# Weight tiles and split buffers of a two-layer decoder: eleven raw tiles and four pairs for the experts, six pairs in the mixers and the dense stage

## The chip, the cores and the metric

The kernel runs on one core of a Trainium2 chip. A core has five engines with queues of their own: TensorE (PE in the profile; PEld are its weight loads, which overlap the matmuls), VectorE (DVE), ScalarE (ACT), GpSimd (POOL) and SyncE (SP), which here issues nearly all DMAs. Each queue runs in order: an instruction that waits holds up everything behind it on its engine. The metric is the time of one execution on the device, in microseconds (us); lower is better.

## The reference

Two layers of a decoder for 256 tokens with 1024 channels, all in float32. Each layer is a mixer stage and a feed-forward stage, each with a residual. What is computed, shortened:

```python
for l in range(2):
    h = rmsnorm(x, norm_mix[l])
    z = h @ w_in[l]                                   # 2816 columns, shared out among four mixers
    y_a, y_b, y_c, y_d = gmlp(z_a), pool(z_b), attention(z_q, z_k, z_v), conv(z_d)
    gates = sigmoid(h @ w_gate[l] + b_gate[l])        # 4 x 1024 columns
    merged = sum(gates[:, b] * (y_b @ w_br[b][l]) for b in "abcd")
    x = x + merged @ w_out[l]
    h = rmsnorm(x, norm_ffn[l])
    if l == 0: f = (silu(h @ w1) * (h @ w3)) @ w2     # dense, 2816 hidden
    else:      f = sum over 8 experts of combine[:, e] * ((silu(h @ w1[e]) * (h @ w3[e])) @ w2[e])
    x = x + f                                         # experts: 3584 hidden, the top 2 of 8 per token
out = rmsnorm(x, norm_final)
```

## The kernel before

**Weights.** All large weights come from HBM in tiles of 1024 KB (128 partitions x 2048 float32, 8 KB per partition), called raw. `load_raw` takes the next tile of a ring and has SP load it. `load_w` does the same and then splits each half of the tile into two parts, whi and wlo (128 x 1024 each): ScalarE copies the half into the reduced float format (`split`, L164), VectorE subtracts the copy from the original (L165). A whi and its wlo make a pair of buffers, also 8 KB per partition. A large product is then three matmuls in the reduced format: hi x whi, hi x wlo and lo x whi (`mm3`, L156 to L158), or two where both parts of the activations stand side by side (`both_parts`, L240 and L242). A raw tile is free again when its two halves are split, a pair when its last matmul is done.

**Rings.** `rawp` has 4 raw tiles (NRAW). The expert stage adds a pool `rawm` of NRAW_MOE = 5, so there its ring has 9. The pool `wp` has 6 pairs, which all stages share; every allocation takes the next of them.

**Stages.** `norm_T` normalises x, two tiles of 128 tokens one after the other (`norm_rows`: squares on ScalarE L200, their sum L201, root L202, reciprocal L204, scaling L207; with the residual's addition L199 ahead of them), and turns the result for TensorE (L217). `mixer_layer` works through 32 tiles of weights: the input projection, 16 gate units (psw), the branches a, b, d and c (psb). Branch c comes last: its two tiles, four pairs, are used for every block of output columns, so all four are held until its end; branch d, just before it, uses two pairs. While it runs, VectorE and ScalarE merge the branch into `merged` and split the result into mp (L564 to L569). `out_proj` follows with four tiles (pso, `rows_by_token_tile`): the first two are used up for both token tiles before the next; the last two are held until the first token tile is finished with both, so that its norm can begin early. `dense_ffn` has 33 tiles (psw for the up products, psf for the down product).

**Experts.** `moe` counts the tokens of each expert and sorts the experts by size. The four larger ones have room for 128 tokens and use split weights; the four smaller ones have room for 64 and multiply in plain float32 straight from the raw tiles, which are held until those matmuls are done. `paired` runs 28 steps, seven for each pair of a larger and a smaller expert. A step takes 12 raw tiles, in this order: two for the first up product of the large expert (psu, L866), two for the down product of the small one two steps back (psds, L944), two for the second up product, four for the small expert's up products (psq, L923; 32 matmuls), two for the large one's down product (psd). Between them stand gfm (L872, L873) and gfs (L925, L926), which apply the activation to psu and psq, and the transposes with their evacuations gTr, gTl and gTs. At each change of pair the inputs of the next two experts are gathered by matmuls (psg, L835), and the results are scattered back (L902). Which expert a tile belongs to is known in advance for the first one alone; for the others SP reads the number from SBUF (L1014) before it can issue the load.

**Order.** The program is traced in the order of the source; then a planner, which simulates the engines and the DMA with costs of its own, puts the instructions of each engine into the order in which they run in this simulation. A split can so run ahead of its place in the source, as soon as the planner believes its tile landed and its pair free. The order is fixed at build time. `hold_splits` (L110) keeps some splits after each norm behind the norm's last instructions; the first two halves are exempt (skip = 2).

**Memory.** Pools are stacked: a pool opened in a stage lies where the pools of the stage before it lay, and with reuse_waits="tile" each tile waits only for the tiles that lay in its place. A stage's pools are closed at its end.

The ring, and the two lines that choose a pair:

```python
ring = {"pools": [rawp] * NRAW, "i": 0, "skip": 0, "after": []}
    hi = wp.tile([P, a // 2, n], F32R, name="whi", tag="whi")
    lo = wp.tile([P, a // 2, n], F32R, name="wlo", tag="wlo")
ring.update(pools=[rawm] * NRAW_MOE + [rawp] * NRAW, i=0)      # in moe, L675
```

Of the kernel before, what the change touches and what calls it, by code (L numbers as in the profile page):

```python
# [11 lines left out]
F32R = mybir.dt.float32r  # L12
# [5 lines left out]
P = 128  # L18
# [11 lines left out]
WINDOWS = (2, 4, 8, 16)  # L30
NSLOT = 128
NRAW = 4
NRAW_MOE = 5
NSMALL = 64
RMS_EPS = 1e-6
LN_EPS = 1e-5
# [59 lines left out]
def decoder_kernel(ctx, tc, x_in, consts_in, mconsts_in, bias_in, small_in, gln_in, gbs_in, norms_in, w_in,  # L96
# [3 lines left out]
    cp = ctx.enter_context(tc.tile_pool(name="cp", bufs=1))  # L100
    actp = ctx.enter_context(tc.tile_pool(name="actp", bufs=1))
    rawp = ctx.enter_context(tc.tile_pool(name="rawp", bufs=NRAW))
    wp = ctx.enter_context(tc.tile_pool(name="wp", bufs=6))
    psA = ctx.enter_context(tc.tile_pool(name="psA", bufs=4, space=bass.MemoryType.PSUM))
    psB = ctx.enter_context(tc.tile_pool(name="psB", bufs=4, space=bass.MemoryType.PSUM))


    ring = {"pools": [rawp] * NRAW, "i": 0, "skip": 0, "after": []}

    def hold_splits(ins, skip):  # L110

# [2 lines left out]
    @contextmanager  # L114
    def behind(ins):
        with ExitStack() as st:
            for i in ins:
                st.enter_context(tc.issue_after(i.ins))
            yield

    def load_raw(src, a, n):
        pool = ring["pools"][ring["i"] % len(ring["pools"])]
        ring["i"] += 1
        raw = pool.tile([P, a, n], F32, name="raw", tag="raw")
        nc.sync.dma_start(raw, src)
        return raw

    def load_w(src, a, n):

        raw = load_raw(src, a, n)
        halves = []
        for i in range(2):
            r = raw[:, i * (a // 2):(i + 1) * (a // 2)]
            hi = wp.tile([P, a // 2, n], F32R, name="whi", tag="whi")
            lo = wp.tile([P, a // 2, n], F32R, name="wlo", tag="wlo")
            with behind(ring["after"] if -6 < ring["skip"] <= 0 else []):
                split(hi, lo, r)
            ring["skip"] -= 1  # L140
            halves.append((hi, lo))
        return halves, a // 2

    def wsl(wt, k, c0, n):
        halves, ah = wt
        return tuple(p[:, k % ah, c0:c0 + n] for p in halves[k // ah])

    def w_cols(w, c0, n):
        return load_w(w[:, c0:c0 + n].rearrange("(k p) n -> p k n", p=P), KD, n)

    def w_rows(w, k0, nk, c0=0, n=D):
        return load_w(w[k0 * P:(k0 + nk) * P, c0:c0 + n].rearrange("(k p) n -> p k n", p=P), nk, n)

    def mm3(ps, lhs, rhs, start, stop):

        nc.tensor.matmul(ps, lhsT=lhs[0], rhs=rhs[0], start=start, stop=False)  # L156
        nc.tensor.matmul(ps, lhsT=lhs[0], rhs=rhs[1], start=False, stop=False)  # L157
        nc.tensor.matmul(ps, lhsT=lhs[1], rhs=rhs[0], start=False, stop=stop)  # L158

    def sl(pair, *idx):  # L160
        return (pair[0][idx], pair[1][idx])

    def split(hi, lo, src):
        return (nc.scalar.activation(hi, src, AF.Copy),  # L164
                nc.vector.tensor_tensor(out=lo, in0=src, in1=hi.bitcast(F32), op=ALU.subtract))  # L165
# [21 lines left out]
    def sqrt_table(after, rows=slice(None)):  # L187

        junk = cp.tile([P, 1], F32, name="junk", tag="junk", bufs=2)
        nc.scalar.activation(junk[rows], after, AF.Sqrt, scale=0.0, bias=eps_l[rows])  # L190
# [53 lines left out]
    def w_pair(h, wt, c=0):  # L244

        out = []
        for b in range(2):
            ps = psA.tile([P, 2, T], F32, name="psw", tag="mm")
            for k in range(KD):
                both_parts(ps, wsl(wt, k, c + b * P, P), h[2], k, k == 0, k == KD - 1)  # L250
            out.append(ps)
        return out

    def addends(pool, ps, out=None):

        if out is None:
            out = pool.tile([P, 2, T], F32, name="sum", tag="sum", bufs=2)
        for b in range(2):
            nc.scalar.activation(out[:, b], ps[b][:, 1], AF.Copy)  # L259
            nc.vector.tensor_tensor(out=out[:, b], in0=out[:, b], in1=ps[b][:, 0], op=ALU.add)  # L260
        return out


    def mixer_layer(l, h):
        with ExitStack() as lctx:
            lp = lctx.enter_context(tc.tile_pool(name=f"lp{l}", bufs=1, reuse_waits="tile"))
            wk = lctx.enter_context(tc.tile_pool(name=f"wk{l}", bufs=2, reuse_waits="tile"))
            sm = lp.tile([P, S_END], F32, name="sm")
# [345 lines left out]
    def out_proj(l, mT):  # L614

        ps = [[psB.tile([P, 512], F32, name=f"pso{t}{n}", tag="ax") for n in range(2)] for t in range(TT)]
        sqrt_table(mT[1].bitcast(F32)[:, KD - 1, 0:1])
        def part(i, wt, t):
            for k in range(2):
                for n in range(2):  # L620
                    mm3(ps[t][n], sl(mT, slice(None), 2 * i + k, slice(t * P, (t + 1) * P)),
                        wsl(wt, k, n * 512, 512), i == 0 and k == 0, i == 3 and k == 1)

        rows_by_token_tile(part, lambda i: w_rows(w_out[l], 2 * i, 2), 4)
        return ps


    def dense_ffn(i, h):
        with ExitStack() as lctx:
            wk = lctx.enter_context(tc.tile_pool(name="wkf", bufs=2, reuse_waits="tile"))  # L630
            ps2 = [[psB.tile([P, 512], F32, name=f"psf{t}{n}", tag="ax") for n in range(2)] for t in range(TT)]
            nch = DFF // 256

            def part(c, wt, g, t):
                for k in range(2):
                    for n in range(2):
                        mm3(ps2[t][n], sl(g, slice(None), k, slice(t * P, (t + 1) * P)),
                            wsl(wt, k, n * 512, 512), c == 0 and k == 0, c == nch - 1 and k == 1)

            def up(c):  # L640
                p1 = addends(wk, w_pair(h, w_cols(dense_w1[i], c * 256, 256)))
                p3 = addends(wk, w_pair(h, w_cols(dense_w3[i], c * 256, 256)))
                sil = wk.tile([P, 2, T], F32, name="sil", tag="sil")
                nc.scalar.activation(sil, p1, AF.Silu)
                if c == nch - 1:
                    sqrt_table(sil[:, 0, 0:1])
                gf = wk.tile([P, 2, T], F32, name="gf", tag="gf")
                nc.vector.tensor_tensor(out=gf, in0=sil, in1=p3, op=ALU.mult)
                g = (wk.tile([P, 2, T], F32R, name="gr", tag="gr"), wk.tile([P, 2, T], F32R, name="gl", tag="gl"))
                split(g[0], g[1], gf)  # L650
                return g

            g = {0: up(0)}
            for c in range(1, nch):
                g[c] = up(c)
                if c < nch - 1:
                    wt = w_rows(dense_w2[i], 2 * (c - 1), 2)
                    for t in range(TT):
                        part(c - 1, wt, g[c - 1], t)
            last = [(c, w_rows(dense_w2[i], 2 * c, 2)) for c in (nch - 2, nch - 1)]  # L660
            for t in range(TT):
                for c, wt in last:
                    part(c, wt, g[c], t)
        return ps2


    def moe(i, norm_i, l, mT):
        with ExitStack() as lctx:
            rawm = lctx.enter_context(tc.tile_pool(name="rawm", bufs=NRAW_MOE, reuse_waits="tile"))
            st = lctx.enter_context(tc.tile_pool(name="stm", bufs=2, reuse_waits="tile"))  # L670
# [3 lines left out]
            ps = out_proj(l, mT)  # L674
            ring.update(pools=[rawm] * NRAW_MOE + [rawp] * NRAW, i=0)  # L675

# [186 lines left out]
            def up_large(e, c, j0, xl):  # L863
                ps = psA.tile([P, 512], F32, name="psu", tag="mm")
                wt = [load_w(tile_of(e, c, j0 + j, 4), 4, 512) for j in range(2)]
                for k in range(KD):  # L866
                    mm3(ps, sl(xl, slice(None), k), wsl(wt[k // 4], k % 4, 0, 512), k == 0, k == KD - 1)
                return ps
# [173 lines left out]
    for l in range(DEPTH):  # L1042
        mT = mixer_layer(l, norm_T(ps, 2 * l))
        if l % 2 == 0:
            ps = dense_ffn(l // 2, norm_T(out_proj(l, mT), 2 * l + 1))
        else:
            moe(l // 2, 2 * l + 1, l, mT)
# [36 lines left out]
def build(tc, ins, outs):  # L1084
    decoder_kernel(tc, *ins.values(), outs["0"])
# [16 lines left out]
```

## Time and profile before

| | |
|---|---|
| median of 3 runs | 1591.19 us (1590.26 to 1591.65) |
| the profiled execution, its own time | 1589.84 us |
| its span, first to last instruction | 1588.1 us |
| granted TensorE clock, mean | 0.988 |
| TensorE busy | 1531.3 us, 96% |
| VectorE, ScalarE busy | 977.8 us, 808.1 us |
| read from HBM | 472.17 MB |

One execution was recorded. A line such as "L165 DVE TENSOR_TENSOR wlo<-raw,whi" names the source line, the engine, the operation, and what it writes and reads; the time in brackets at the end of a timeline row is how long the engine sat idle before it, and what ended this. Matmuls overlap in the array, so their start times, not their durations, tell the pace.

### The profile page before, as it was taken

Reading aid. Unit: us, or ns where it says so; the run is one execution under the profiler, and the core shown is the slowest. Engines: PE = TensorE matmul, PEld = TensorE weight load, DVE = VectorE, ACT = ScalarE, POOL = GpSimd, SP = SyncE. Lnnn points to the kernel's source line nnn. Section 1 sums busy time; section 2 is a strip of 40 time slices with the busy share of each in tenths; the row PEclk is TensorE's granted clock in tenths of the full one; section 3 lists DMA queues with packets and bytes.
Section 4 is the critical chain, followed back from the end, with each engine's and each line's share of the span. In section 5 each row is a group of like instructions: output and inputs, shape, how many; then the busy total and the mean of one; then the engine's idle time right before and its main releaser. Section 6 shows DMA issues by size and latency. Waiting matters only on the chain.

```text
span 1588.1 us, 20024 instructions
## 1 busy us (share of the span) xinstructions
PE 1531.3 (96%) x7508; PEld 1065.8 (67%) x7508; DVE 977.8 (62%) x1291; ACT 808.1 (51%) x1184; POOL 20.8 (1%) x47
## 2 busy tenths in 40 slices
PE   6999999999899999899999999999999999999997
PEld 5888897888788889776555555555555555555553
DVE  5896776665679777765445655454645554654444
ACT  5577746555464865554434534344434453444342
POOL 2000000000100000000000000000000000000000
PEclk9999999999999999989999999999999999999998
DMA  9565555555565645479998989999999999899993
GB/s 324 189 192 181 173 181 173 187 188 190 186 199 167 198 160 196 163 307 376 421 407 371 413 343 421 400 413 374 385 372 403 404 408 373 365 417 405 398 390 141
DMA packets 134890, 474.61 MB, mean 299 GB/s; under 512 B 7744, under 2 KB 77376, under 8 KB 91776
## 3 DMA queue, kind: packets, MB, share of 16 engines
q1 hardware_dynamic: 132512, 466.65, 76.2%
q0 software_dynamic: 1984, 6.08, 1.2%
q8 instruction: 61, 1.00, 0.3%
q10 hardware_dynamic: 288, 0.52, 0.1%
q14 instruction: 45, 0.37, 0.1%
HBM read 472.17 MB, written 1.05 MB: 298 GB/s over the span
## 4 chain that ended last, share of the span: by engine, by line
PE 89%; DVE 4%; ACT 4%; issue 2%; DMA 1%; SPq 0%; DVEq 0%; ACTq 0%
PE psw L240 16%; PE psq L923 14%; PE psw L242 8%; PE psu L157 7%; PE psu L158 7%; PE psu L156 6%; PE psds L944 5%; PE psd L157 3%; ACT whi L164 3%; PE psd L158 3%; DVE wlo L165 3%; PE psd L156 2%; PE psg L835 2%; PE psf L156 1%; PE psf L158 1%
## 5 line engine op out<-in xcount | busy, mean ns | idle before, releaser
L165 DVE TENSOR_TENSOR wlo<-raw,whi 128x1024 fp32r<-128x1024 f32 x546 | 647.7, 1221 | 252.8 <-ACT whi L164 249.6
L164 ACT ACTIVATE whi<-raw 128x1024 fp32r<-128x1024 f32 x546 | 554.0, 1053 | 130.4 <-PE psw L240 40.1
L240 PE MATMUL psw<-hp,whi 128*128 128x512 f32 x1088 | 388.6, 400 | 0.6 <-DVE hp L165 0.6
L242 PE MATMUL psw<-hp,wlo 128*128 128x256 f32 x1088 | 307.0, 282 | 0.0
L240 PEld LDWEIGHTS psw<-hp,whi 128*128 128x128 f32 x1088 | 205.1, 188 | 52.8 <-issue 3.3
L923 PE MATMUL psq<-raw,xs 128*64 128x512 f32 x896 | 218.6, 596 | 0.0
L242 PEld LDWEIGHTS psw<-hp,wlo 128*128 128x128 f32 x1088 | 206.3, 190 | 2.1 <-issue 1.1
L157 PE MATMUL psu<-wlo,xer 128*128 128x512 f32 x448 | 183.4, 409 | 9.5 <-DVE wlo L165 9.5
L156 PE MATMUL psu<-whi,xer 128*128 128x512 f32 x448 | 179.6, 401 | 1.3 <-DVE x L902 1.2
L158 PE MATMUL psu<-whi,xel 128*128 128x512 f32 x448 | 176.1, 393 | 0.0
L923 PEld LDWEIGHTS psq<-raw,xs 128*64 128x64 f32 x896 | 65.3, 137 | 129.0 <-issue 128.7
L925 ACT ACTIVATE gfs<-psq 64x512 f32<-64x512 f32 x28 | 16.5, 591 | 251.7 <-PE psq L923 251.7
L157 PEld LDWEIGHTS psu<-wlo,xer 128*128 128x128 f32 x448 | 84.6, 189 | 64.0 <-issue 30.0
L156 PEld LDWEIGHTS psu<-whi,xer 128*128 128x128 f32 x448 | 84.8, 189 | 41.9 <-ACT whi L164 17.0
L944 PE MATMUL psds<-raw,gTs 128*64 128x512 f32 x448 | 110.8, 604 | 0.0
L926 DVE TENSOR_TENSOR gfs<-gfs,psq 64x512 f32<-64x512 f32 x28 | 19.4, 692 | 137.7 <-ACT gfs L925 137.7
L158 PEld LDWEIGHTS psu<-whi,xel 128*128 128x128 f32 x448 | 84.8, 189 | 15.3
L157 PE MATMUL psd<-wlo,gTr 128*128 128x512 f32 x224 | 92.3, 412 | 2.1
L158 PE MATMUL psd<-whi,gTl 128*128 128x512 f32 x224 | 88.1, 393 | 0.0
L259 ACT ACTIVATE sum<-psw 128x256 f32<-128x256 f32 x120 | 44.8, 374 | 67.0 <-PE psw L242 67.0
L156 PE MATMUL psd<-whi,gTr 128*128 128x512 f32 x224 | 75.4, 413 | 2.7 <-ACT whi L164 2.7
L872 ACT ACTIVATE gfm<-psu 128x512 f32<-128x512 f32 x28 | 16.7, 597 | 119.9 <-PE psu L158 119.9
(260 smaller groups left out, 1570.4 us busy)
## 6 DMA issues: line engine op xcount, KB each, us to landing
raw<-in_moe_w_dram SPq DMA_DIRECT2D x336, 1024.0 KB, 8.2
raw<-in_dense_w_dram SPq DMA_DIRECT2D x33, 1024.0 KB, 5.3
raw<-in_w_gate_dram SPq DMA_DIRECT2D x32, 1024.0 KB, 5.4
raw<-in_w_in_dram SPq DMA_DIRECT2D x22, 1024.0 KB, 5.6
raw<-in_w_out_dram SPq DMA_DIRECT2D x8, 1024.0 KB, 5.0
raw<-in_w_br_c_dram SPq DMA_DIRECT2D x4, 1024.0 KB, 5.5
s<-in_bias_dram POOLq DMA_DIRECT2D x16, 192.0 KB, 4.2
gain<-in_norms_dram SPq DMA_DIRECT2D x5, 512.0 KB, 4.9
```

The costliest lines, as they stand in the source:

```text
L156: nc.tensor.matmul(ps, lhsT=lhs[0], rhs=rhs[0], start=start, stop=False)
L157: nc.tensor.matmul(ps, lhsT=lhs[0], rhs=rhs[1], start=False, stop=False)
L158: nc.tensor.matmul(ps, lhsT=lhs[1], rhs=rhs[0], start=False, stop=stop)
L164: return (nc.scalar.activation(hi, src, AF.Copy), nc.vector.tensor_tensor(out=lo, in0=src, in1=hi.bitcast(F32), op=ALU.subtract))
L165: nc.vector.tensor_tensor(out=lo, in0=src, in1=hi.bitcast(F32), op=ALU.subtract))
L240: nc.tensor.matmul(ps.rearrange("p a t -> p (a t)"), lhsT=w[0], rhs=act[:, k].rearrange("p a t -> p (a t)"), start=start, stop=False)
L242: nc.tensor.matmul(ps[:, 1], lhsT=w[1], rhs=act[:, k, 0], start=False, stop=stop)
L259: nc.scalar.activation(out[:, b], ps[b][:, 1], AF.Copy)
L835: nc.tensor.matmul(ps[:, b, cs], lhsT=ht[part][:, t, k * P:(k + 1) * P], rhs=self.G[:, t].rearrange("p s n -> p (s n)")[:, cs], start=n == ...
L923: nc.tensor.matmul(ps[rows], lhsT=xs[:, kk], rhs=w[:, k], start=kk == 0, stop=kk == KD - 1)
L926: nc.vector.tensor_tensor(out=gf[HI], in0=gf[HI], in1=ps[HI], op=ALU.mult)
L944: nc.tensor.matmul(acc["s"][rows], lhsT=gT[:, 2 * j + k], rhs=w[:, k, n * 512:(n + 1) * 512], start=c == 0 and j == 0 and k == 0, stop=c = ...
```

## The change

The experts' pool of raw tiles grows from 5 to 7, so the ring there has 11 tiles instead of 9. The pool `wp` shrinks from 6 pairs to NW = 4. `mixer_layer` and `dense_ffn` each open a pool of two further pairs for as long as they run (`more_parts`), so the ring of pairs has 6 there and 4 elsewhere: in the experts and in both output projections. The position in the ring of pairs is now counted by `ring["n"]`, which starts at 0 when such a pool opens and when it closes. The memory is the same: two raw tiles take as much as two pairs.

```diff
-NRAW_MOE = 5
+NRAW_MOE = 7
+NW = 4
...
-    wp = ctx.enter_context(tc.tile_pool(name="wp", bufs=6))
+    wp = ctx.enter_context(tc.tile_pool(name="wp", bufs=NW))
...
-    ring = {"pools": [rawp] * NRAW, "i": 0, "skip": 0, "after": []}
+    ring = {"pools": [rawp] * NRAW, "i": 0, "skip": 0, "after": [], "parts": [wp] * NW, "n": 0}
+
+    def more_parts(lctx, name):
+
+        pool = lctx.enter_context(tc.tile_pool(name=name, bufs=2, reuse_waits="tile"))
+        ring.update(parts=[wp] * NW + [pool] * 2, n=0)
+        lctx.callback(lambda: ring.update(parts=[wp] * NW, n=0))
...
-            hi = wp.tile([P, a // 2, n], F32R, name="whi", tag="whi")
-            lo = wp.tile([P, a // 2, n], F32R, name="wlo", tag="wlo")
+            pool = ring["parts"][ring["n"] % len(ring["parts"])]
+            ring["n"] += 1
+            hi = pool.tile([P, a // 2, n], F32R, name="whi", tag="whi")
+            lo = pool.tile([P, a // 2, n], F32R, name="wlo", tag="wlo")
...
     def mixer_layer(l, h):
         with ExitStack() as lctx:
+            more_parts(lctx, f"wp{l}")
...
     def dense_ffn(i, h):
         with ExitStack() as lctx:
+            more_parts(lctx, "wpf")
```

## The prediction

> **What bounds the kernel now.** The page comes first: the span, the engines' busy time, and the slices.
>
> ```profile
> span 1588.1 us, 20024 instructions
> PE 1531.3 (96%) x7508; PEld 1065.8 (67%) x7508; DVE 977.8 (62%) x1291; ACT 808.1 (51%) x1184; POOL 20.8 (1%) x47
> PE   6999999999899999899999999999999999999997
> DMA  9565555555565645479998989999999999899993
> ```
>
> TensorE is busy nearly throughout, and from slice 18 on (the experts) the DMA engines are too. Either could pace the experts, so the next view is the table by stretch. Its columns are the stretch, its length, busy us of PE, PEld, DVE, ACT and POOL, the granted clock, the DMA share and GB/s.
>
> ```profile
> 655.00:675.00 20.00, 14.87 (x94) 12.45 (x93) 14.56 (x40) 8.83 (x18) 0.00 (x0) 0.83 0.07 27
> 688.00:703.00 15.00, 15.00 (x65) 12.34 (x65) 11.97 (x11) 12.27 (x13) 0.00 (x0) 0.97 0.60 222
> 703.00:737.00 34.00, 34.00 (x155) 21.72 (x153) 19.37 (x19) 16.27 (x19) 0.00 (x0) 1.00 1.01 414
> 797.00:829.00 32.00, 31.09 (x131) 17.37 (x130) 15.88 (x15) 13.54 (x16) 0.00 (x0) 1.00 1.01 420
> ```
>
> At 420 GB/s a raw tile (1024 KB, 1.049 MB) takes 2.50 us, and the 12 tiles of a step 30.0 us. How long is a step? The chain of waits, in order of time, shows the bursts of small-expert matmuls (psq), one burst per step (start, us, what):
>
> ```profile
> 708.65 7.02 PE psq L923 x32
> ...
> 737.09 7.02 PE psq L923 x32
> ...
> 766.79 7.01 PE psq L923 x30
> ...
> 1218.18 7.03 PE psq L923 x30
> ...
> 1249.83 7.01 PE psq L923 x30
> ```
>
> The first whole step takes 737.09 - 708.65 = 28.44 us, the next 29.70, a settled one 1249.83 - 1218.18 = 31.65. So a settled step is 1.65 us longer than its tiles need and 3.2 longer than TensorE alone once needed. Does it wait for tiles? The waits say (us in total, times, longest):
>
> ```profile
> ACT gfs L925 <- PE psq L923: 251.7, 28, 11.8
> ...
> ACT whi L164 <- DMA raw<-in_moe_w_dram: 20.4, 11, 5.2
> ...
> PE psu L157 <- DVE wlo L165: 9.5, 16, 0.6
> ```
>
> Only 11 splits of 336 waited for a landing, 20.4 us in all, and that is ScalarE's idle time, not TensorE's. The wait of 251.7 us is of another kind, and one step of ScalarE's queue in the timeline shows it:
>
> ```profile
> 1209.09 4.93 ACT L164 ACTIVATE whi<-raw 128x1024 fp32r<-128x1024 f32 x5
> 1225.23 0.59 ACT L925 ACTIVATE gfs<-psq 64x512 f32<-64x512 f32 x1 [11.20 <-PE psq L923]
> 1225.84 2.95 ACT L164 ACTIVATE whi<-raw 128x1024 fp32r<-128x1024 f32 x3
> ```
>
> Five splits are done by 1214.02: four for the second up product and the first of the down product. The down product's other three stand behind gfs, which waits 11.20 us for the psq burst, although the second of them reads the tile that the first has read already. The order was written by the planner, and it is this order, with the switches between psq and psu that go with it, that makes 31.65 of 28.44: neither a missing raw tile nor a missing buffer.
>
> **The change, part by part.** No instruction is added or removed. What moves are buffers, and the planner's order where it depends on them.
>
> (1) Eleven raw tiles and four buffer pairs for the experts. A large tile fills two pairs, so the stock that can be loaded ahead is 9 + 6/2 = 12 tiles before and 11 + 4/2 = 13 after: one tile more, not two. At the start of the stage it counts as follows, in SP's queue:
>
> ```profile
> 627.56 13.90 SPq L125 DMA_DIRECT2D raw<-in_moe_w_dram  x8
> ...
> L1014 SPq TENSOR_LOAD <-ixi x7: 262/262/474, 670.7 to 674.4; - x7
> ...
> 675.15 2.22 SPq L125 DMA_DIRECT2D raw<-in_moe_w_dram  x4
> ...
> 691.48 6.84 SPq L125 DMA_DIRECT2D raw<-in_moe_w_dram  x3
> ```
>
> Eight loads go out early. The ninth is a small expert's, whose number comes from the register loads of L1014, so SP cannot pass 674.4 however many tiles are free: in 655 to 675 the DMA share of 0.07 stays. Four loads follow, then SP waits for a tile until 691.48. After the change a fifth goes with the four (13 tiles), and each later load leaves when its predecessor left before: the stream is one tile, 2.5 us, ahead. Bounds of the gain: 2.5 us if the steps are paced by landings to the end, 0 if they are not. The settled steps are not, by the 20.4 us; the first ones partly are (share 1.01 in 703 to 737). I take one more step at the pace of the first, 29.70 - 28.44 = 1.26: **-1.3 us**.
>
> By the Trainium skill ("DMA: Bandwidth & Descriptors", Bandwidth) loads from HBM are bound by some 358 GB/s per core; that would make 12 tiles 35.1 us, the stream would pace every step, more tiles could gain only the head start, and this term would be -2.9 us (an estimate from that page). The trace disagrees with 420 GB/s, beside a ceiling of 435 that the same section gives for the ports.
>
> (2) Four pairs inside a step. A part serves six matmuls; on the quoted seam below two of them start 0.23 us apart, so 1.38 us per part. With four pairs a split may begin when the part four earlier is used up and is needed three parts later, 4.1 us. It takes a copy and a subtraction:
>
> ```profile
> L165 DVE TENSOR_TENSOR wlo<-raw,whi 128x1024 fp32r<-128x1024 f32 x546 | 647.7, 1221 | 252.8 <-ACT whi L164 249.6
> L164 ACT ACTIVATE whi<-raw 128x1024 fp32r<-128x1024 f32 x546 | 554.0, 1053 | 130.4 <-PE psw L240 40.1
> ```
>
> 1.05 + 1.22 = 2.3 us, leaving 1.8. The cover is TensorE's own work on the three parts between. Bounds: 0, and, if one more operation of VectorE (0.69 us) and the wait for its turn eat the margin, some 0.3 us per step, 8 in 28 steps. Nearest row: TensorE waited 9.5 us in all for wlo in the up product. I take 0.
>
> (3) Output projections run outside the mixers and the dense stage, so with four pairs too. The last branch (c) holds four parts to its end; before, the other two pairs (branch d's) were free for the first tile of w_out. The end of branch c in layer 1, queues of ScalarE, VectorE and TensorE:
>
> ```profile
> 622.89 2.01 ACT L164 ACTIVATE whi<-raw 128x1024 fp32r<-128x1024 f32 x2 [2.10 <-PE psb L157]
> ...
> 633.54 2.01 ACT L164 ACTIVATE whi<-raw 128x1024 fp32r<-128x1024 f32 x2 [2.44 <-PE psb L157]
> ```
>
> ```profile
> 634.67 0.69 DVE L564 SCALAR_TENSOR_TENSOR mtmp<-gate,psb 128x512 f32<-128x512 f32 x1 [0.93 <-PE psb L158]
> 635.28 1.22 DVE L165 TENSOR_TENSOR wlo<-raw,whi 128x1024 fp32r<-128x1024 f32 x1
> ...
> 637.01 1.22 DVE L165 TENSOR_TENSOR wlo<-raw,whi 128x1024 fp32r<-128x1024 f32 x1
> ```
>
> ```profile
> 634.36 0.28 PE L158 MATMUL psb<-ycr,wlo 128*128 128x256 f32 x1
> 634.47 0.39 PE L156 MATMUL pso<-whi,mp 128*128 128x512 f32 x1
> 634.70 0.40 PE L157 MATMUL pso<-wlo,mp 128*128 128x512 f32 x1
> ```
>
> The pair of splits at 622.89 is w_out's first tile, those at 633.54 its second; psb runs into pso without a gap. Afterwards the first tile stands where the second stood. whi is there at 634.6, and four matmuls (both token tiles, both halves) run on it, to 635.5; wlo ends at 635.28 + 1.22 = 636.5. TensorE waits 1.0 us; the second wlo (638.2) arrives while the first's eight matmuls and the next four run (12 x 0.23 = 2.8, to 639.3). Bounds: 0, if the planner puts the subtraction ahead of mtmp and uses other work, and 2.3, the whole split. I take 0.9 in each of two layers: **+1.8**. The remaining tiles have 11 us of matmuls (48 x 0.23) before them and stay covered.
>
> (4) The first tile after a projection is no longer split in the middle of it but when the projection's third tile frees its pairs, in the last quarter, beside the norm of the first token tile. In layer 0:
>
> ```profile
> 235.12 0.17 DVE L204 RECIPROCAL rs<-ss 128x1 f32<-128x1 f32 x1 [0.36 <-ACT ss L202]
> 235.32 1.41 DVE L207 SCALAR_TENSOR_TENSOR hh<-x,rs,gain 128x512 f32<-128x512 f32 x2
> 237.59 1.37 DVE L199 TENSOR_TENSOR x<-x,pso 128x512 f32<-128x512 f32 x2 [0.86 <-PE pso L158]
> ```
>
> VectorE has 0.86 us free before L199, a subtraction takes 1.22 and comes before or in L204's place; the second waits behind L207. What is late is the norm's second half, and behind it the transposes and TensorE. Bounds 0 and 2.1 (two subtractions less the gap, and ScalarE's share); I take 0.9, one subtraction's overhang and ScalarE's delay. In layer 1 ScalarE's copy is already in that place:
>
> ```profile
> 656.51 1.06 ACT L164 ACTIVATE whi<-raw 128x1024 fp32r<-128x1024 f32 x1 [0.31 <-PE pso L158]
> 657.47 0.61 ACT L200 ACTIVATE hhm<-x 128x512 f32<-128x512 f32 x1
> ```
>
> The squares (L200) already wait for it, so up to 1.0 us of delay on VectorE is covered; without that cover 1.2. I take 0. Together **+0.9**.
>
> (5) Mixers and dense stage. Six pairs as before, with the rotation starting at the same pair in each stage; the two pairs of the new pool lie where branch d's weights or the dense stage's lay, free long before. 0, and if the pool's opening made its first split wait for the stage before, one split, 2.3, at three places.
>
> **Sum:** -1.3 + 1.8 + 0.9 = +1.4 us on the profiled execution's 1589.84 (its span is 1588.1, with 1.7 around it): 1591.2. The median of the three runs, 1591.19, is 1.35 above the profiled execution, so 1592.6.
>
> **Rivals.**
> A, faster: the greater stock changes the planner's order. If a larger reserve lets the down product's splits go ahead of gfs, a step falls from 31.65 towards 30.0, what its tiles need: at most 24 settled steps x 1.65 = 40 us. More likely it holds for one step after the start and after each of the three changes of expert pair, where TensorE works without weights: 4 x 3.2 = 12.8 less the seams' 2.7: -10, 1581. For it: the clean step at 708.65, while the reserve lasted. Against it: the tiles land in time in settled steps too.
> B, slower: four pairs are too few inside a step. The down product is followed at once by the next up product; eight parts are 8 x 1.38 = 11.0 us on TensorE and 8 x 1.22 = 9.8 on VectorE, where two further operations of 0.69 for gfs and gTl make 11.2. Where this comes to more than TensorE's time, each step loses the difference and its share of the wait: 0.3 x 28 = 8, with the seams 1601; it decides from the point at which more than 1.8 us of other work stands ahead of a split. Against it: 16 waits of at most 0.6 us.
> C, the forecast: no change that can be measured, only seams and start.
>
> **Chances.** C 0.40, A 0.32, B 0.28. A measurement of this kernel tells about 0.2% (3.2 us) from no change, so same is 1588.0 to 1594.4, which is also C's own range; faster 0.32, same 0.40, slower 0.28. The range over the cases runs from a little past A's 1581 to B's 1601, 1579 to 1601: beyond it lie A's full 40 us and B with all upper bounds at once, about 2 in 10.
>
> **What would show it.** Step 1: SP's loads after the register loads come as a group of five, and the step from the first psq burst to the third is some 1 us shorter; wrong if more than five go or the settled steps leave 31 to 31.65. Step 2: the wait of psu and psd for wlo stays near 10 us in all; more than 20 speaks for B. Step 3: pso's first matmuls show a wait for wlo of about 1 us in both layers, and the splits at 622.89 are gone. Step 4: a wlo between L201 and L199 of the norm in layer 0. The prediction falls if bursts of 32 psq matmuls become the rule (A), or if TensorE's idle time in settled steps grows (B).

## The result, and the profile after

The changed kernel takes **1612.07 us** (median of four runs, 1610.82 to 1613.05), the kernel before 1591.42 in the same comparison: a ratio of 1.0131, 95% interval 1.0113 to 1.0148. That is 20.7 us slower, where 1592.6 was forecast, and outside the range of 1579 to 1601.

The profiled execution took 1610.82 us, its span 1609.1. The page of the changed kernel: span, busy time, and the slices of TensorE and the DMA engines.

```profile
span 1609.1 us, 20107 instructions
PE 1546.4 (96%) x7508; PEld 1068.9 (66%) x7508; DVE 980.7 (61%) x1291; ACT 811.2 (50%) x1184; POOL 20.3 (1%) x47
PE   6999999999899999899999999999999999999997
DMA  9656545665565557179999989999989999799992
```

The same 7508 matmuls keep TensorE busy for 15.1 us longer (1546.4 against 1531.3), and only some 6 of the 21 us are new idle time. So the question is not only who waits for whom, but why the same work takes longer. The tables by stretch show where (columns as in the prediction). The stretches are: first projection; norm until the dense stage's first down product; from there to the second projection; second projection; norm and router until the first gather; the first two expert steps; the step with the second change of pair; the one with the third. Before:

```profile
216.30:238.20 21.90, 21.90 (x100) 18.09 (x99) 15.47 (x19) 11.48 (x17) 0.00 (x0) 1.00 0.59 193
238.20:268.80 30.60, 26.81 (x145) 23.28 (x144) 20.99 (x30) 19.86 (x31) 0.00 (x0) 0.89 0.53 170
268.80:634.50 365.70, 361.38 (x2067) 309.74 (x2066) 262.23 (x401) 214.77 (x354) 6.82 (x14) 1.00 0.57 185
634.50:656.40 21.90, 21.90 (x100) 18.09 (x99) 15.50 (x19) 14.44 (x20) 0.90 (x1) 1.00 0.71 286
656.40:669.30 12.90, 7.78 (x61) 5.64 (x59) 8.07 (x25) 6.70 (x14) 0.00 (x0) 0.96 0.11 42
...
683.70:744.10 60.40, 60.40 (x262) 39.76 (x262) 35.33 (x33) 31.88 (x35) 0.00 (x0) 0.96 0.82 328
...
1126.00:1162.70 36.70, 34.37 (x146) 19.18 (x145) 26.52 (x29) 18.40 (x22) 0.00 (x0) 1.00 0.82 336
...
1352.40:1386.70 34.30, 33.12 (x146) 19.35 (x145) 24.35 (x27) 15.95 (x20) 0.00 (x0) 1.00 0.88 360
```

After:

```profile
216.10:239.20 23.10, 22.37 (x96) 17.86 (x96) 15.46 (x17) 13.03 (x17) 0.00 (x0) 1.00 0.58 183
239.20:272.10 32.90, 27.36 (x145) 23.33 (x146) 22.90 (x35) 20.27 (x32) 0.00 (x0) 0.90 0.58 192
272.10:639.50 367.40, 363.06 (x2067) 310.68 (x2065) 260.34 (x400) 212.92 (x353) 6.79 (x14) 0.99 0.58 189
639.50:662.50 23.00, 22.31 (x96) 17.84 (x96) 15.39 (x16) 13.52 (x18) 0.90 (x1) 1.00 0.47 185
662.50:678.60 16.10, 9.41 (x61) 6.71 (x60) 10.18 (x29) 7.18 (x16) 0.00 (x0) 0.87 0.09 34
...
693.10:759.40 66.30, 66.30 (x262) 39.69 (x262) 38.42 (x35) 34.21 (x37) 0.00 (x0) 0.96 0.85 335
...
1141.40:1180.30 38.90, 36.26 (x146) 20.50 (x146) 26.80 (x29) 18.70 (x22) 0.00 (x0) 0.96 0.79 316
...
1369.70:1408.60 38.90, 36.26 (x145) 20.45 (x145) 26.80 (x29) 18.68 (x22) 0.00 (x0) 0.96 0.79 319
```

The projections cost 1.2 and 1.1 us more, what follows them 2.3 and 3.2, the mixers between 1.7: about 9.5. The first two expert steps cost 5.9 more and two changes of pair 2.2 and 4.6; the rest of the experts gives 1 back.

Up to 6.5 us of this, an estimate from the rows, go with the granted clock, the column behind POOL's. Length times the missing share gives 2.1 us in the norm and router (0.13 x 16.1) where 0.5 were lost before, and 1.6 at each of the two changes of pair (0.04 x 38.9) where nothing was. In the stretch of the mixers the trace shows 6.8 us at a clock of 0.50 instead of 3.4, which is 1.7 us. The four executions after had a mean clock of 0.981 to 0.983, the 51 of the kernel before in these comparisons 0.984 to 0.989. No run separates whether the longer waits bring the clock down or only the moments at which they fall. The 5.9 us of the first two steps have nothing to do with it: the clock is 0.96 before and after.

**The experts.** In the first two steps TensorE is busy without a gap before and after, with the same 262 matmuls, and yet 5.9 us longer. The timeline of TensorE after, in the first step, shows what has become of the burst that was one of 32 rows and 7.02 us (708.65 in the prediction; line numbers differ between the kernels, L934 here is the L923 of before):

```profile
711.56 2.79 PE L934 MATMUL psq<-raw,xs 128*64 128x512 f32 x10
...
715.31 0.40 PE L167 MATMUL psu<-whi,xel 128*128 128x512 f32 x1
715.64 1.07 PE L934 MATMUL psq<-raw,xs 128*64 128x512 f32 x2
716.64 0.49 PE L166 MATMUL psu<-wlo,xer 128*128 128x512 f32 x1
716.97 0.39 PE L167 MATMUL psu<-whi,xel 128*128 128x512 f32 x1
...
720.73 2.79 PE L934 MATMUL psq<-raw,xs 128*64 128x512 f32 x10
...
723.88 1.93 PE L934 MATMUL psq<-raw,xs 128*64 128x512 f32 x6
...
727.10 1.08 PE L934 MATMUL psq<-raw,xs 128*64 128x512 f32 x4
```

Each psq product (64 columns) shows as two rows. Two rows take 1.07 us and four rows 1.08: two products, one for each half of the columns, run at the same time, and one alone takes as long as both. Six rows take 1.93, ten 2.79: an odd product costs a whole place of 0.86 us. The 16 products took 7.02 us in one burst; in pieces of 5, 1, 5, 3 and 2 they take 2.79 + 1.07 + 2.79 + 1.93 + 1.08 = 9.66. In the two steps together psq takes 18.0 us instead of 14.2, and psds, in pieces of 10 and 6 rows, 4.7 instead of 3.7: 4.9 of the 5.9 us. And the change between products of 128 and of 64 columns has a price: around the single product the rows start 0.33 us apart (715.31 to 715.64, 716.64 to 716.97), where 0.23 is the rule. From the psu product at 715.31 to that at 716.97 pass 1.66 us, 1.20 more than the two places of 0.23 that they need.

This is in accord with what the Trainium skill ("TensorEngine Tiling (Array Packing)", Key Properties) says: tiles of the array work in parallel, and a change of the tiling mode drains TensorE.

At the second change of pair most of the 2.2 us is the clock. At the third the clock is 1.6 of the 4.6 us, TensorE waits 1.5 longer (38.90 - 36.26 against 34.30 - 33.12), and psds there ends in pieces of 6 and 2 rows instead of 8.

Why in pieces? The planner writes them. That it puts small products where it expects a large one to wait for its split part is the likely reason, but no run shows its estimates. What four pairs do is seen on ScalarE, in its waits for pairs that psu uses, before and in the changed kernel, and in TensorE's wait for parts (us in total, times, longest):

```profile
ACT whi L164 <- PE psu L158: 15.9, 20, 2.4
```

```profile
ACT whi L173 <- PE psu L167: 68.7, 59, 5.3
...
PE psu L166 <- DVE wlo L174: 8.9, 15, 0.6
```

ScalarE waits 68.7 us for such a pair to come free (15.9 before), TensorE in psu no more for wlo than before (9.5).

**The projections.** In the list of what uses pso, TensorE's idle time is

```profile
its engine sat idle before it (us, times) until:
  DVE wlo L174: 1.4, 2
```

0.7 us in each of the two projections, where there was none. Behind it stands a larger loss. VectorE and ScalarE after, at the end of the second projection (L208 adds a token tile's sums, L216 scales):

```profile
658.94 1.29 DVE L208 TENSOR_TENSOR x<-x,pso 128x512 f32<-128x512 f32 x2 [0.40 <-PE pso L167]
661.37 1.23 DVE L174 TENSOR_TENSOR wlo<-raw,whi 128x1024 fp32r<-128x1024 f32 x1 [1.14 <-ACT whi L173]
662.51 0.68 DVE L208 TENSOR_TENSOR x<-x,pso 128x512 f32<-128x512 f32 x1
...
664.88 1.42 DVE L216 SCALAR_TENSOR_TENSOR hhm<-x,rs,gain 128x512 f32<-128x512 f32 x2
```

```profile
659.66 0.64 ACT L209 ACTIVATE hhm<-x 128x512 f32<-128x512 f32 x1 [2.38 <-DVE x L208]
...
660.29 1.04 ACT L173 ACTIVATE whi<-raw 128x1024 fp32r<-128x1024 f32 x1
661.24 0.62 ACT L209 ACTIVATE hhm<-x 128x512 f32<-128x512 f32 x1
```

The same of VectorE before:

```profile
650.33 1.37 DVE L199 TENSOR_TENSOR x<-x,pso 128x512 f32<-128x512 f32 x2 [2.38 <-PE pso L158]
...
653.84 1.42 DVE L207 SCALAR_TENSOR_TENSOR hhm<-x,rs,gain 128x512 f32<-128x512 f32 x2
```

The first token tile's sums are added 3.6 us before the projection's end (before: 6.1 us), because TensorE, short of parts of the fourth weight tile, works ahead on the second token tile (with its order held they are added 5.8 us before the end again, in a run below). Then a whi stands between that token tile's squares and a wlo between its adds and its scaling, which begins 5.9 us after the first add instead of 3.5.

### The profile page after: what moved, and what is told of

Read it like the earlier page. It is cut to its first block, busy times and chain, and to the rows that moved or that the text cites. A ratio compares the mean times of both kernels' runs of the same rounds, so it can differ in the third digit from the quotient of the medians.

```text
span 1609.1 us, 20107 instructions
## 1 busy us (share of the span) xinstructions
PE 1546.4 (96%) x7508; PEld 1068.9 (66%) x7508; DVE 980.7 (61%) x1291; ACT 811.2 (50%) x1184; POOL 20.3 (1%) x47
## 5 line engine op out<-in xcount | busy, mean ns | idle before, releaser
L173 ACT ACTIVATE whi<-raw 128x1024 fp32r<-128x1024 f32 x546 | 557.8, 1054 | 166.8 <-PE psu L167 68.7
L934 PE MATMUL psq<-raw,xs 128*64 128x512 f32 x896 | 222.7, 597 | 0.0
L934 PEld LDWEIGHTS psq<-raw,xs 128*64 128x64 f32 x896 | 65.5, 137 | 129.0 <-issue 128.4
L884 DVE TENSOR_TENSOR gfm<-gfm,psu 128x512 f32<-128x512 f32 x28 | 19.2, 687 | 93.0 <-PE psu L167 92.7
```

The costliest lines, as they stand in the source:

```text
L173: return (nc.scalar.activation(hi, src, AF.Copy), nc.vector.tensor_tensor(out=lo, in0=src, in1=hi.bitcast(F32), op=ALU.subtract))
L884: nc.vector.tensor_tensor(out=gf, in0=gf, in1=p3, op=ALU.mult)
L934: nc.tensor.matmul(ps[rows], lhsT=xs[:, kk], rhs=w[:, k], start=kk == 0, stop=kk == KD - 1)
```

## The experiments

The first four put back or take alone one part of the change. Three theories: **S**, the projections lose; **P**, four pairs lose inside the experts; **R**, the raw tiles matter.

**Six pairs in both projections again**, the rest as changed:

```
def out_proj(l, mT):
+    with ExitStack() as octx:
+        more_parts(octx, f"wpo{l}", n=4)
+        return projection(l, mT)
```

> Eleven raw tiles and four pairs in the experts as in the change, but both output projections get six pairs again (the two further pairs lie where the mixers' lay). Theory S (the seams): the trace of the changed kernel has 9.3 of its 21 us before the first up product of the experts; those go, so about 1603, and if the rest of the loss comes from the late start and the altered plan after it, 1592. Theory P (four pairs cost inside the experts): the 11 to 12 us behind the first up product stay, 1602 to 1604. Theory R (the raw tiles help and the seams alone hurt): 1588.

1600.2 us (1598.74 to 1600.61), ratio 1.005 [1.0031, 1.0069]: 8.8 us of the loss stay.

**The same with nine raw tiles** (a tile that nothing reads keeps the place of the two others):

```
-ring.update(pools=[rawm] * NRAW_MOE + [rawp] * NRAW + [rawx] * 2, i=0)
+ring.update(pools=[rawm] * NRAW_MOE + [rawp] * NRAW, i=0)
```

> As the run with six pairs in the projections, but with nine raw tiles: only the experts' four pairs are left of the change. Theory P: as with eleven raw tiles or up to one tile (2.5 us) longer, 1602 to 1607. Theory S: 1592. Theory R: raw tiles are worth 2.5 us or more, so it is longer than the run with eleven by that.

1602.18 us (1599.35 to 1603.21), 1.0063 [1.0041, 1.0084]. By the medians the two raw tiles are worth some 2 us with four pairs, but the intervals overlap: this is not shown.

**Four pairs in the projections alone**, experts as before:

```
 ps = out_proj(l, mT)
+ring.update(parts=six, n=0)   # experts: six pairs, nine raw tiles
```

> Only the seams of the change: four pairs in both output projections, and in the experts nine raw tiles and six pairs as before. Theory S: 1600 to 1612, the start of the first up product some 9 us late as in the changed kernel. Theory P: what the trace of the changed kernel shows before the experts, 1600 to 1601, and the steps after it as before. If the lateness were only a changed clock, less than 1596.

1600.27 us (1599.14 to 1602.21), 1.0052 [1.0032, 1.0073]: 8.9 us. With the 8.8 above this is 17.7 of the 20.7: both halves of the loss stand alone and nearly add.

**The exchange the other way**, seven raw tiles and eight pairs in the experts, six elsewhere:

```
-NRAW_MOE = 7
-NW = 4
+NRAW_MOE = 3
+NW = 6        # and two pairs more in the experts
```

> The opposite exchange: six pairs everywhere, in the experts eight pairs and seven raw tiles. Theory P: pairs are what the steps lack, so the first steps and the changes of pair get shorter, 1580 to 1588. Theory R: raw tiles are what counts, so 1596 or more. If neither matters in that direction, 1590 to 1593.

1595.31 us (1592.17 to 1597.6), 1.0024 [1.0013, 1.0035]: slower too, by 3.9. Theory P falls: more pairs do not help. Theory R's 1596 is nearly reached, so that two raw tiles fewer cost these 3.9 us is not excluded by this run.

The second group tests the order of the small products directly, without a buffer changed. **psq behind the step's last psu, in the first two steps only** (on the kernel with eleven raws, four pairs in the experts, six in the projections):

```
+with behind([marks["up"]] if s < 3 else []):   # marks["up"]: the last psu product
     gfs = up_small(place_of[npair + pr1], c1, slots[pr1].xs)
```

> Eleven raw tiles, four pairs in the experts, six pairs in both projections (as in the run with the projections undone, 1600.2 us), and one order more: in the first two expert steps the small expert's up products (psq) stand behind the step's last psu on TensorE. Theory O (with four pairs the written order cuts psq into pieces of 10, 2, 10, 6 and 4 rows between psu; a piece of an odd number of products leaves half of TensorE's columns empty once, and psq and psds of the first two steps took 18.0 + 4.7 us instead of 14.2 + 3.7): psq back at 14.2 us, the stretch from the first psu to the end of the second psq from 65.7 to about 61, in all about 1596. Theory W (the pieces only fill time in which TensorE would wait for the four pairs): psq at 14.2 us too, but as much idle time before psu, and 1599 to 1601.

1592.38 us (1590.61 to 1595.89), 1.0011 [1.0002, 1.0021]: by the medians 7.8 of the 8.8 us come back, more than expected. Not all of it is the order. The two profiled executions differ by 5.8 us: 3.9 in the first two steps (65.7 to 61.8), as theory O said, and 2.0 in the mixers, which the edit does not touch and where the earlier run spent 10.2 us at a clock of 0.50, this one 3.4. The first step's burst is whole again:

```profile
708.81 7.09 PE L941 MATMUL psq<-raw,xs 128*64 128x512 f32 x32
```

**The same in every step**:

```
-behind([marks["up"]] if s < 3 else [])
+behind([marks["up"]] if s < steps else [])
```

> As the run before it, with the order in every expert step. In settled steps the written order puts one psq product (2 rows) before the last five of psu, and psq takes 8.2 us instead of 7.1 (about 18 of 28 steps). Theory O: 18 x 1.1 = 20 us less than 1596, so 1576 to 1580. Theory W: the single product fills a wait for a split part, which then stands open: 1596 to 1601.

1570.07 us (1569.11 to 1572.19), 0.9867 [0.985, 0.9883], below theory O's range and better than the kernel before.

**The kernel before with that order** (the same two lines):

> The kernel before (nine raw tiles, six pairs) with that order in every step. Theory O: its 18 steps with a psq of 2 and 30 rows lose 1.1 us each, 1572 to 1576. Theory W: 1590 to 1593. If this gains as much as the same order with four pairs does, the order has nothing to do with the number of pairs in settled steps, and only the first steps and the changes of pair tell four from six.

1569.64 us (1566.82 to 1570.37), 0.9854 [0.9837, 0.987]: 21.2 us faster, some 2 more than expected, and the same time as with eleven raw tiles and four pairs. The groups by line, psq before and here (count, busy, mean ns, idle before):

```profile
L923 PE MATMUL psq<-raw,xs 128*64 128x512 f32 x896 | 218.6, 596 | 0.0
...
L944 PE MATMUL psds<-raw,gTs 128*64 128x512 f32 x448 | 110.8, 604 | 0.0
```

```profile
L157 PE MATMUL psu<-wlo,xer 128*128 128x512 f32 x448 | 181.8, 406 | 9.5 <-DVE wlo L165 9.5
...
L923 PE MATMUL psq<-raw,xs 128*64 128x512 f32 x896 | 198.4, 595 | 0.0
```

218.6 - 198.4 = 20.2 us of the 21.2. A step with pieces of 2 and 30 rows takes 1.07 + 7.08 us for psq, one whole burst 7.09, so this is 19 steps with one product alone. Theory W, that the single product filled a real wait, falls: the wait of psu for wlo is 9.5 us with and without it.

**psds held too**, behind the last psu of the step's first half:

```
+with behind([marks["up"]] if s < steps else []):
     down_small(place_of[npair + pr2], c2, gTs)
```

> The kernel before with psq held in every step (1569.6 us), and the small expert's down products (psds) held too, behind the last psu of the step's first half, so that they stand as one piece of 16 rows. Theory O: psds from 110.8 to 28 x 3.66 = 102 us, and the three changes of pair lose 1 to 2.5 us each: 1559 to 1563. Theory W (the pieces of psds fill the wait for the last split part of the first half, which then stands open): 1566 to 1571.

**1549.51 us** (1548.24 to 1551.02), 0.9734 [0.9717, 0.9751]: 2.7% faster than the kernel before, and 10 us more than expected.

```profile
L156 PE MATMUL psu<-whi,xer 128*128 128x512 f32 x448 | 180.0, 402 | 4.0 <-DVE x L902 4.0
L157 PE MATMUL psu<-wlo,xer 128*128 128x512 f32 x448 | 177.6, 396 | 0.0
...
L944 PE MATMUL psds<-raw,gTs 128*64 128x512 f32 x448 | 103.0, 599 | 0.0
```

psds gives 7.8 us (110.8 to 103.0), and the wait of psu for wlo, 9.5 us, is gone, with 4.2 us of busy time (181.8 to 177.6); psu waits 2.7 us more for x at the changes of pair. That is 18.8 of the 20.1 us. So this wait had been made by the pieces of psds. A step of the kernel before lets one see how:

```profile
1205.27 1.94 PE L944 MATMUL psds<-raw,gTs 128*64 128x512 f32 x8
...
1208.60 0.60 ACT L872 ACTIVATE gfm<-psu 128x512 f32<-128x512 f32 x1 [5.29 <-PE psu L158]
...
1211.45 0.50 PE L157 MATMUL psu<-wlo,xer 128*128 128x512 f32 x1 [0.60 <-DVE wlo L165]
```

The piece at 1205.27 stands ahead of the last five products of the step's first half. It keeps them back, and with them gfm and the splits behind it on ScalarE (from 1209.09, in the prediction), for the first of which psu then waits.

**Eleven raws and four pairs with both small products held** (six pairs in the projections):

> Eleven raw tiles and four pairs in the experts, six pairs in the projections, and both small products held (psq behind the step's last psu, psds behind the last psu of its first half). With nine raws and six pairs the two orders gave 1549.5 us. Theory O (between four and six pairs only the written order of the small products differs): the same order, so 1548 to 1552. Theory P (four pairs are late by themselves): 1555 or more, with new waits of psu for wlo or whi, since no piece of psds or psq fills them.

1548.63 us (1548.04 to 1549.53), 0.9735 [0.9719, 0.9751]. With the order held, eleven raw tiles with four pairs and nine with six take the same time in the experts, and TensorE's wait of psu for wlo, theory P's sign, is 0.0.

The last group belongs to the projections. **Four pairs there, token tile 1's products with the last two weight tiles behind token tile 0's:**

```
 for t in range(TT):
+    with behind([end] if end is not None else []):
         for i, wt in last:
-            part(i, wt, t)
+            end = part(i, wt, t)
```

> Four pairs in the projections, experts as before (the run with only that was 1600.3 us), and one order more: token tile 1's products with the last two weight tiles stand behind token tile 0's on TensorE. Theory S1 (four pairs cost there because TensorE works ahead on token tile 1, so that token tile 0's sums end late and its norm has nothing beside it): the first residual add of layer 0 from 235.6 to 232 to 233.5, of layer 1 some 5 us earlier in its projection, in all 1593 to 1596. Theory S2 (the fourth weight tile's parts themselves are late by that much, whichever way the products stand): TensorE waits inside the projection instead, and 1599 to 1602.

1596.47 us (1594.58 to 1598.2), 1.0034 [1.0025, 1.0044]: 3.8 of the 8.9 us come back. **Six pairs with the plain order of the four weight tiles**, so that token tile 0's sums end late without any shortage:

```
-rows_by_token_tile(part, lambda i: w_rows(w_out[l], 2 * i, 2), 4)
+for i in range(4):
+    wt = w_rows(w_out[l], 2 * i, 2)
+    for t in range(TT):
+        part(i, wt, t)
```

> The kernel before with the plain order in both output projections: both token tiles of a weight tile, one weight tile after another, so that 12 products (2.9 us) of token tile 1 instead of 24 (5.8 us) follow token tile 0's last. No wait for a pair is added. Theory S1 (what four pairs cost in the projections is mostly that token tile 0's norm has less beside it): up to 2.9 us at each of the two projections, 1593 to 1597. Theory S2 (it is the wait for the split parts): 1590 to 1592.

1591.96 us (1589.84 to 1594.03), 1.0003 [0.9994, 1.0013]: S2's number, no difference, although token tile 0's sums are added only 3.4 us before the projection's end. So S1 as written is not borne out. From the second projection's end to the first gather, with the order held at four pairs, and with the plain order at six:

```profile
660.20:673.70 13.50, 8.25 (x61) 5.76 (x60) 9.38 (x26) 6.92 (x14) 0.00 (x0) 1.00 0.10 40
```

```profile
658.20:671.20 13.00, 7.78 (x62) 5.90 (x61) 9.65 (x28) 6.71 (x14) 0.00 (x0) 0.97 0.12 42
```

13.5 and 13.0 us against 16.1 in the changed kernel and 12.9 before. Late sums alone cost nothing here, splits beside early sums 0.6; both together cost 3.2. The clock is a third candidate: it is 1.00 and 0.97 in these two rows, 0.96 before and 0.87 in the changed kernel, where the same 61 products keep TensorE busy for 1.6 of the 3.2 us longer (9.41 against 7.78). (In layer 0 the plain order's stretch is 32.9 us, as long as after the change, at a clock of 0.84; the medians do not show it.) To move the splits alone, **the two early splits of the first expert tile were put behind the norm's end** in layer 1, with four pairs:

```
+norm_end = [last, root]      # token tile 1: last scaling, square root
-behind(ring["after"] if -6 < ring["skip"] <= 0 else [])
+behind(ring["after"] if -6 < ring["skip"] <= 0 else ring["early"] if ring["skip"] > 0 else [])
```

> Four pairs in the projections only (as in the run of 1600.3 us), and in layer 1 the two splits of the first expert weight tile that may go early stand behind token tile 1's last scaling on VectorE and its last square root on ScalarE. Token tile 0's sums stay as late as they are. Theory S3 (it takes both, late sums of token tile 0 and splits that stand in the middle of its norm): from the last product of the second projection to the first gather product 13 to 14 us instead of 16.8, and 1596.5 to 1598. Theory S4 (the late sums alone): 16 to 17 us, and 1599.5 to 1601.

1602.89 us (1600.18 to 1605.09), 1.007 [1.0052, 1.0088], by the median neither theory's number. Two of the four executions took 1600.2 and 1600.9 us, S4's number, at a mean clock of 0.985 to 0.986; the two others, and the profiled one is among them, took 1605 at 0.981. In the profiled one ScalarE shows a new stall:

```profile
666.57 3.88 ACT L173 ACTIVATE whi<-raw 128x1024 fp32r<-128x1024 f32 x4
670.36 1.55 ACT L705 ACTIVATE hTm<-pt 128x512 f32<-128x512 f32 x3
```

Four whi now stand as a block before the copies (hTm) that the router needs, and the stretch to the first gather grows from 16.8 to 19.7 us, at a clock of 0.72 instead of 0.81. The run moved the stall instead of taking it away, so it does not decide between S3 and S4. That four pairs in the projections cost 8.9 us is shown, and that the order of the products gives 3.8 of it back; how the loss behind the projections divides between the splits, the late sums and the clock is open.

**The changed kernel with psq held and the projections ordered:**

> The changed kernel (eleven raw tiles, four pairs, also in the projections) with both orders: psq behind the step's last psu in every expert step, and token tile 1's products with the last two weight tiles behind token tile 0's. Theory O with S1: 1570 (eleven raws and four pairs with psq held and six pairs in the projections) and 4 to 6 us for what the ordered projections with four pairs still cost (1596.5 against 1590.8): 1573 to 1577, 15 us faster than the kernel before, and 3 to 7 slower than the same order with nine raws and six pairs (1569.6). A rival, that four pairs cost by themselves once nothing fills their waits: 1580 or more.

1579.79 us (1578.74 to 1581.74), 0.9929 [0.9911, 0.9946]: 32.3 us faster than the changed kernel, some 3 slower than expected, and 10 slower than the kernel before with the same order of psq. 5.7 of these 10 are the projections (the ordered run above); the rest was not traced to one place. The rival's 1580 lies within the scatter of this run; what speaks against it are the runs with six pairs in the projections, where four pairs in the experts cost nothing once the order is held.

Eleven raw tiles together with six pairs were not run, so what the two raw tiles alone would do to the kernel before is not known.

## Why the prediction was wrong

**What bounds the kernel** was read rightly, and more than its own sum made of it. It said that "this order, with the switches between psq and psu that go with it" makes a settled step longer. The runs with the order held give 21 and, with psds, 42 us. The sign stood in its own lines: bursts of x32 in the first two steps, of x30 in the later ones, whose missing product stands alone. But the change was then priced by its waits, and its effect on the order only as a possible gain (rival A).

**Step 1**, -1.3: the five loads went as foreseen:

```profile
684.68 2.62 SPq L132 DMA_DIRECT2D raw<-in_moe_w_dram  x5
```

The stretch behind the first two steps, up to the first change of pair, is 1.9 us shorter (155.7 against 157.6), near the size forecast. The loss elsewhere hides it, the runs with nine and eleven raw tiles do not separate it from their scatter (1602.18 and 1600.2), and once the order is held nothing is left to be told apart (1549.51 and 1548.63).

**Step 2, "I take 0", is the step that failed** for the experts: measured 8.8 us. Its sign (the wait for wlo near 10 us) came out as predicted, 8.9, and was the wrong sign to look for. Four pairs do not make TensorE wait longer in psu; with them the planner cuts the small products, and odd pieces leave half of the columns empty. Rival B's 8 us for the experts come near the 8.8 by luck: it wanted 0.3 us in each of 28 steps, while 5.9 us sit in the first two steps and the rest at the changes of pair, part of it clock.

**Step 3**, +0.9 at each projection: 1.2 and 1.1, with the wait for wlo of 0.7 each. The mechanism and nearly the size were right. "The remaining tiles ... stay covered" was not: TensorE kept busy by working ahead on token tile 1.

**Step 4**, +0.9 in layer 0 and 0 in layer 1, failed too: 2.3 and 3.2. In layer 0 it looked for a wlo behind the first token tile's sum (L201) and took only the norm's second half to be late. In the trace the wlo, at 238.02, stands ahead of that sum, at 239.76, and the scaling begins 5.4 us after the first add instead of 3.2: the first half is late too. The cover that it named in layer 1, the squares that wait for a whi anyway, was sized for token tile 0's sums 6.1 us before the projection's end. With 3.6 us it is gone, and 1.6 of the 3.2 us go with TensorE's longer busy time at the lower clock, a term that the sum did not have.

**Step 5**, 0: the mixers are 1.7 us longer, with a granted clock of 0.99 instead of 1.00 in that stretch, which accounts for it; no wait of the opening pool showed.

## What to carry to other kernels

When a planner writes the order, a change of buffers is a change of order: compare the pieces in which each engine's products stand before and after, not only the waits. Matmuls that use half of the columns belong together, and a piece of them should have an even count: one lone product cost 1.2 us with its two switches. Here a one-line order constraint was worth more than any division of the memory that was run. Splits of the next stage's weights that come free late can land in the norm between the stages. And before a difference of a few microseconds is put down to a change, compare the granted clock stage by stage.

## What the runs showed of the hardware

The granted clock fell to half after a stretch in which TensorE was partly busy. At the third change of pair in the changed kernel, the 3.41 us ahead of the fall, with the small experts' sums (pssc), and the 3.41 us behind it, with psu products (length, busy us of TensorE, granted clock, DMA share, GB/s):

```profile
1391.15:1394.56 3.41, 2.06 (x10) 1.00 0.81 255
1394.56:1397.97 3.41, 3.41 (x10) 0.50 1.03 435
```

TensorE was busy for 2.06 of 3.41 us; then the psu products start some 0.42 us apart instead of 0.23, and 1.7 us are lost. By the Trainium skill ("TensorE: Matmul & The Clock Gate", What's actually happening) the clock halves after an idle window of some 3.4 us, in a window that runs free of the kernel; the trace shows that a window in which TensorE was busy for 60% can be enough. It is not always enough: in 660.69 to 664.10 of the same trace it was busy for 1.84 us, and the clock stayed at 1.00 for the next 3.4 us. The fall comes at the second and the third change of pair after and at none before. It does not need four pairs: the kernel before with psq held has one at its first change of pair (at 922.53, after 2.11 busy us of 3.41).

In the kernel before the first gathers of the experts' inputs (psg, 669.30 to 683.70) ran at a granted clock of 0.50 throughout, although TensorE shows as busy for 14.39 of the 14.40 us; why is open. Executions of that kernel alone reach from 1588.6 us at a mean clock of 0.989 to 1594.7 at 0.984.
